# Dilated attention on one core: 64-row products and values' products as runs, PSUM banks shared otherwise

## The chip, the core and the metric

The kernel runs on one core of a Trainium2 chip. A core has a matrix engine (TensorE, PE here; its weight loads are shown apart as PEld), a vector engine (VectorE, DVE), a scalar engine (ScalarE, ACT), a general one (GpSimd, POOL) and one that issues transfers (SyncE, SP). Each takes its instructions in the order in which the program holds them and waits on semaphores. PE reads SBUF and writes PSUM, which has eight banks of 128 x 512 fp32. The metric is the device time of one execution in microseconds.

## The reference, cut to what matters

One decoder layer over 512 tokens of width 1024, in fp32: half a SwiGLU FFN, then three gated branches (an S5 state space model, causal dilated attention, cross attention into 256 memory tokens), an output projection, and a second half FFN. The change is in the dilated attention, and in the tags of the banks that the other two branches use.

```python
HEAD_DIM = 64
ATTN_PATTERNS = ((128, 1), (512, 4), (2048, 16))
HEADS_PER_PATTERN = 4

def dilated_mixture_attention(q, k, v, rel_table):
    ...
        logits = jnp.einsum('bqghd,bgqkhd->bghqk', qb, kb) * scale + bias[None, :, :, None, :]
        logits = jnp.where(valid[None, :, None], logits, -jnp.inf)
        lse = jax.nn.logsumexp(logits, axis=-1)
        probs = jnp.exp(logits - lse[..., None])
        out = jnp.einsum('bghqk,bgqkhd->bqghd', probs, vb)
        mix = jax.nn.softmax(lse, axis=1)
        return jnp.einsum('bghq,bqghd->bqhd', mix, out).astype(q.dtype)
```

The mixture over the three patterns, weighted by their softmax denominators, is one softmax over all keys of the three patterns together, and the kernel computes it so.

## The kernel before, in words

Tokens are held in residue order: token 4j + r stands at place j of block r, so a query tile is one of four blocks of 128 tokens (`r`), and the dilated patterns become dense products on blocks with a mask in the bias. Heads go in pairs (`hp`, two pairs): head 2hp lies on partitions 0 to 63, head 2hp + 1 on 64 to 127 of the transposed queries and keys. So there are eight tiles, `attn_tile(hp, r)`, of two heads each.

For one head of one tile, PE makes scores in two banks: `s0` (512 keys of the first pattern, by L856 over all 128 rows and L857 over the head's 64 rows, which adds the low part of the keys) and `s1` (128 keys of each of the other patterns, two products at L860 over 64 rows; an fp32 product shows as two passes in the profile). DVE adds the bias and takes the row maximum (L864, L866), L758 negates it, ACT takes the exponential with its sum (L762), DVE the reciprocal and the scaled row (L764, L765). PE transposes the row in six pieces of 128 (L873) into two banks, four pieces and two, and ACT copies them to `pt` (L874). When both heads have their `pt`, twelve products (L880), six key blocks times two heads, add up 64 columns each in `pacc`: one head's output on partitions 0 to 63, the other's on 64 to 127.

Between tiles, the program has the gated linear unit of the SSM branch and its gate (`up_block`, `gate_T`, with `mm_T`, L133 to L135): products of 128 rows by 512 columns, whose weights ACT and DVE split into high and low parts (L124, L125). After the eighth tile follow the gate of the attention branch and the product of its output `ath`/`atl` (`pacc`, split by L143 and L144) with `attn_w_up`.

PSUM, in this half of the kernel (`ps_open("ps_b", 2)`), has two banks each under the tags `mm`, `tr`, `sc` and `acc`. A tile under a tag waits until the one that held its bank before has been read.

The order of instructions on each engine is not that of the source. A scheduler takes, engine by engine, what it holds ready in a timeline of its own, with source order as priority; then the order is fixed, and an engine that meets a wait lets nothing by. `tc.issue_after(last)`, in the change, tells it to place an instruction behind another one.

Of the kernel before, what the change touches and what calls it, by code (L numbers as in the profile page):

```python
# [20 lines left out]
P = 128  # L21
T = 512
# [5 lines left out]
NEG = -1.0e30  # L28
# [56 lines left out]
def kernel(ctx, tc, x, mem, ffn1_norm, ffn1_w_in, ffn1_w_down, mix_norm, w_in, a_re, a_im, log_dt,  # L85
# [3 lines left out]
    V, S, G, TE = nc.vector, nc.scalar, nc.gpsimd, nc.tensor  # L89
# [570 lines left out]
    def ssm_units(pool, hd):  # L660

        MUL, ADD, SUB = ALU.mult, ALU.add, ALU.subtract
        for i in range(4):
# [16 lines left out]
            yield  # L680
            br = ps_tile("tr", 2)
            bi = ps_tile("tr", 2)
            for part, b in enumerate((br, bi)):
# [38 lines left out]
    def ssm_out(pool, i, stk, lt, ca, xr, xi):  # L722


        py = ps_tile("acc", 2)
        for q in range(4):
# [97 lines left out]
    def xattn_head(pool, hd, xq, mkT, mv):  # L824
        pts = [pool.tile([P, 2, T], F32R, name=f"xpt{z}", tag=f"xpt{z}", bufs=1) for z in "hl"]
        for r in range(4):
            s = ps_tile("sc", 2)
            tok = slice(r * P, (r + 1) * P)
            for i, (a, b) in enumerate(((0, 0), (0, 1), (1, 0))):
                TE.matmul(s[:, :256], xq[a][:, tok], mkT[hd][:, b], start=i == 0, stop=i == 2)  # L830
            mx = pool.tile([P, 1], F32, name="xmx", tag="xmx", bufs=2)
            V.tensor_reduce(mx, s[:, :256], axis=AX.X, op=ALU.max)
            pr = softmax_rows(s[:, :256], mx, pool, 128.0 ** -0.5, 256, "xa")
            pt = ps_tile("tr", 2)
            for kt in range(2):
                TE.transpose(pt[:, kt * P:(kt + 1) * P], pr[:, kt * P:(kt + 1) * P], ident)
            split_plain(pt[:, :256].rearrange("p (k q) -> p k q", k=2), pts[0][:, :, tok], pts[1][:, :, tok])
        po = ps_tile("tr", 2)
        cols = slice((hd % 2) * P, (hd % 2 + 1) * P)
# [8 lines left out]
    def attn_tile(pool, hp, r, qT, kT, v, bias, pacc):  # L848

        tok = slice(r * P, (r + 1) * P)  # L850
        pts = []
        for h in (2 * hp, 2 * hp + 1):
            rows = slice(64 * (h % 2), 64 * (h % 2) + 64)
            s0 = ps_tile("sc", 2)
            qs, (kh, kl) = qT[hp][h % 2], kT[hp]
            TE.matmul(s0, qs[:, tok], kh[h % 2], start=True, stop=False)  # L856
            TE.matmul(s0, qs[rows, tok], kl[rows, :], start=False, stop=True)  # L857
            s1 = ps_tile("sc", 2)
            for p in range(2):
                TE.matmul(s1[:, p * P:(p + 1) * P], qT[2 * p + 2 + hp][rows, tok], kT[2 * p + 2 + hp][rows, tok],  # L860
                          start=True, stop=True)
            sb = pool.tile([P, 6 * P], F32, name="sb", tag="sb", bufs=3)
            mx = pool.tile([P, 2], F32, name="amx", tag="amx", bufs=3)
            V.tensor_tensor_reduce(sb[:, :T], s0, bias[h][:, (3 - r) * P:(7 - r) * P], scale=1.0, scalar=NEG,  # L864
                                   op0=ALU.add, op1=ALU.max, accum_out=mx[:, 0:1])
            V.tensor_tensor_reduce(sb[:, T:], s1[:, :256], bias[h][:, 7 * P:9 * P], scale=1.0, scalar=mx[:, 0:1],  # L866
                                   op0=ALU.add, op1=ALU.max, accum_out=mx[:, 1:2])
            pr = softmax_rows(sb, mx[:, 1:2], pool, 1.0, 6 * P, "at", pr=sb)
            pt = pool.tile([P, 6, P], F32, name="pt", tag="pt", bufs=4)
            for b0, nb in ((0, 4), (4, 2)):  # L870
                ta = ps_tile("tr", 2)
                for b in range(nb):
                    TE.transpose(ta[:, b * P:(b + 1) * P], pr[:, (b0 + b) * P:(b0 + b + 1) * P], ident)  # L873
                S.activation(pt[:, b0:b0 + nb, :], ta[:, :nb * P].rearrange("p (k q) -> p k q", k=nb), AF.Copy)  # L874
            pts.append(pt)
        for b in range(6):
            for h in (2 * hp, 2 * hp + 1):
                rows = slice(64 * (h % 2), 64 * (h % 2) + 64)
                kt, c = (b, h * 64) if b < 4 else (r, (b - 3) * 256 + h * 64)
                TE.matmul(pacc[rows, tok], v[kt][:, c:c + 64], pts[h % 2][:, b, :], start=b == 0, stop=b == 5)  # L880

# [111 lines left out]
    with sb_pool("att") as ap:  # L993
# [8 lines left out]
        for hp in range(2):  # L1002
            pacc = ps_tile("acc", 2)
            for r in range(4):
# [304 lines left out]
```

## Time and profile before

| | |
|---|---|
| three runs | 1272.08 to 1273.12 us, median 1272.59 us |
| profiled execution | 1273.29 us, span 1271.5 us |
| PE busy | 1249.1 us, 98% of the span |
| DVE busy | 800.6 us, 63% |
| ACT busy | 474.9 us, 37% |
| chain that ended last | PE 92%, DVE 4%, DMA 2%, ACT 1% |
| attention stage | 654 to 804 us of the span |

Times in the profile are microseconds from the span's start. A row of a timeline has start, duration, engine, line, operation, output and inputs by the program's names, rows*columns of PE's array in use, shape and count; equal instructions that follow each other are one row. A row of a windows view has, for PE, PEld, DVE, ACT and POOL, busy time and count, then the clock granted to PE (1.00 is full), the share of time that the transfer engines were busy, and GB/s. A bracket at a row's end holds idle time ahead of it and what ended it.

### The profile page before, as it was taken

What the parts mean: (1) busy time and instruction counts of PE and PEld (TensorE: products, weight loads), DVE (VectorE), ACT (ScalarE), POOL (GpSimd) and SP (SyncE); (2) the same over time, 40 slices, a digit from 0 to 9 for tenths busy, and PEclk for the clock granted to TensorE, in tenths of its full rate; (3) what the DMA queues carried; (4) which work ended last, traced back from release to release, by engine and by line L of the source; (5) the groups of instructions that cost most, each with busy time, mean ns of one, the idle gap of its engine ahead of it and who ended that gap; (6) DMA issues with size and microseconds to landing.
All of it is one profiled execution on the core that took longest, in us unless ns stands there. A gap on an engine that the chain in (4) does not pass through costs nothing.

```text
span 1271.5 us, 17256 instructions
## 1 busy us (share of the span) xinstructions
PE 1249.1 (98%) x6764; PEld 1058.3 (83%) x6764; DVE 800.6 (63%) x1519; ACT 474.9 (37%) x744; POOL 104.8 (8%) x85
## 2 busy tenths in 40 slices
PE   8999999999999999999999999999998999999997
PEld 6788888788889788998877777888888899899896
DVE  7999456876547567745535455455588558558564
ACT  4322222233325333224423443334356335335343
POOL 3000000000012033420000000002200001001002
PEclk9999999999999999999999999999998999999999
DMA  6233333654227835652127221334645556556411
GB/s 198 86 114 117 132 106 103 174 162 148 94 88 247 262 117 171 176 169 81 53 70 152 67 67 42 100 108 142 185 105 130 144 152 163 141 149 168 132 66 67
DMA packets 167368, 163.60 MB, mean 129 GB/s; under 512 B 28244, under 2 KB 150676, under 8 KB 166996
## 3 DMA queue, kind: packets, MB, share of 16 engines
q1 hardware_dynamic: 134032, 138.20, 34.8%
q0 software_dynamic: 9632, 9.70, 5.2%
q10 hardware_dynamic: 23624, 14.61, 3.9%
q8 instruction: 53, 0.87, 0.3%
q14 instruction: 27, 0.22, 0.1%
HBM read 147.51 MB, written 16.16 MB: 129 GB/s over the span
## 4 chain that ended last, share of the span: by engine, by line
PE 92%; DVE 4%; DMA 2%; ACT 1%; issue 0%; SPq 0%; ACTq 0%
PE ps_mm L133 19%; PE ps_mm L135 19%; PE ps_mm L134 19%; PE ps_mm L1151 5%; PE ps_mm L1153 5%; PE ps_mm L1154 5%; PE ps_mm L1209 3%; PE ps_mm L1211 3%; PE ps_mm L1210 3%; DMA wraw<-in_xattn_w_kv_dram 1%; PE ps_acc L880 1%; DVE wl L125 1%; PE ps_mm L818 1%; PE ps_mm L817 1%; PE ps_mm L819 1%; PE ps_tr L873 1%
## 5 line engine op out<-in xcount | busy, mean ns | idle before, releaser
L124 ACT ACTIVATE wh<-wraw 128x1024 fp32r<-128x1024 f32 (+2 forms) x224 | 209.4, 937 | 482.3 <-PE ps_mm L134 347.2
L125 DVE TENSOR_TENSOR wl<-wraw,wh 128x1024 fp32r<-128x1024 f32 (+2 forms) x224 | 248.0, 1109 | 130.4 <-ACT wh L124 124.3
L133 PE MATMUL ps_mm<-uh,wh 128*128 128x512 f32 x736 | 289.9, 394 | 0.9 <-ACT uh L143 0.5
L134 PE MATMUL ps_mm<-ul,wh 128*128 128x512 f32 x736 | 288.2, 392 | 1.6 <-DVE ul L144 1.6
L135 PE MATMUL ps_mm<-uh,wl 128*128 128x512 f32 x736 | 288.5, 392 | 0.0
L133 PEld LDWEIGHTS ps_mm<-uh,wh 128*128 128x128 f32 x736 | 138.7, 188 | 30.7 <-issue 1.0
L134 PEld LDWEIGHTS ps_mm<-ul,wh 128*128 128x128 f32 x736 | 138.7, 188 | 30.6 <-DVE ul L144 1.9
L135 PEld LDWEIGHTS ps_mm<-uh,wl 128*128 128x128 f32 x736 | 138.5, 188 | 29.9 <-issue 0.7
L217 POOL TENSOR_TENSOR sqacc<-sqacc,sqk 128x512 f32<-128x512 f32 x12 | 20.1, 1678 | 694.5 <-ACT sqk L216 694.4
L125 DVE TENSOR_TENSOR wl<-s,wh 128x1024 fp32r<-128x1024 f32 x36 | 44.0, 1224 | 43.1 <-ACT wh L124 43.1
L134 PE MATMUL ps_mm<-gl,wh 128*128 128x512 f32 x176 | 70.0, 398 | 0.0
L133 PE MATMUL ps_mm<-gh,wh 128*128 128x512 f32 x176 | 69.9, 399 | 0.0
L135 PE MATMUL ps_mm<-gh,wl 128*128 128x512 f32 x176 | 69.8, 399 | 0.0
L1210 PE MATMUL ps_mm<-wl,gh 128*128 128x512 f32 x176 | 69.4, 394 | 0.0
L1211 PE MATMUL ps_mm<-wh,gl 128*128 128x512 f32 x176 | 69.1, 394 | 0.0
L1209 PE MATMUL ps_mm<-wh,gh 128*128 128x512 f32 x176 | 66.9, 395 | 0.0
L1151 PE MATMUL ps_mm<-uh,wh 128*128 128x256 f32 x216 | 61.1, 285 | 2.3 <-ACT uh L143 1.7
L124 ACT ACTIVATE wh<-s 128x1024 fp32r<-128x1024 f32 x36 | 38.2, 1061 | 64.3 <-PE ps_mm L1153 26.7
L1153 PE MATMUL ps_mm<-ul,wh 128*128 128x256 f32 x216 | 61.4, 285 | 0.7 <-DVE ul L144 0.7
L1154 PE MATMUL ps_mm<-uh,wl 128*128 128x256 f32 x216 | 61.0, 284 | 0.0
L143 ACT ACTIVATE gh<-ff_t 128x512 fp32r<-128x512 f32 x44 | 27.1, 626 | 56.7 <-DVE ff_t L312 33.4
L1151 PEld LDWEIGHTS ps_mm<-uh,wh 128*128 128x128 f32 x216 | 41.2, 191 | 2.9 <-ACT uh L143 2.1
(388 smaller groups left out, 2410.4 us busy)
## 6 DMA issues: line engine op xcount, KB each, us to landing
wraw<-in_ffn_w_in_dram SPq DMA_DIRECT2D x33, 1024.0 KB, 5.1
wraw<-in_w_in_dram SPq DMA_DIRECT2D x25, 1024.0 KB, 5.4
wraw<-in_ffn_w_down_dram SPq DMA_DIRECT2D x12, 768.0 KB, 4.3
s<-in_ffn_w_in_dram SPq DMA_DIRECT2D x18, 512.0 KB, 5.3
s<-in_ffn_w_in_dram POOLq DMA_DIRECT2D x18, 512.0 KB, 6.2
wraw<-in_ffn_w_down_dram SPq DMA_DIRECT2D x8, 1024.0 KB, 5.1
wraw<-in_ffn_w_down_dram SPq DMA_DIRECT2D x10, 512.0 KB, 3.5
q<-in_ffn_w_in_dram SPq DMA_DIRECT2D x9, 512.0 KB, 4.6
```

The lines of the kernel that those rows point to most:

```text
L124: S.activation(h, raw, AF.Copy)
L125: eng.tensor_tensor(l, raw, h.bitcast(F32), op=ALU.subtract)
L133: TE.matmul(ps, h[:, k, :], rhs[k][0], start=first and k == 0, stop=False)
L134: TE.matmul(ps, h[:, k, :], rhs[k][1], start=False, stop=False)
L135: TE.matmul(ps, l[:, k, :], rhs[k][0], start=False, stop=last and k == n - 1)
L143: S.activation(h, src, AF.Copy)
L1151: TE.matmul(o, h[:, k, cols], rhs[k][0], stop=False, **st)
L1153: TE.matmul(o, h[:, k, cols], rhs[k][1], stop=False, **st)
L1154: TE.matmul(o, l[:, k, cols], rhs[k][0], stop=k == 3, **st)
L1209: TE.matmul(pd[r], gh[:, tok], h, start=st, stop=False)
L1210: TE.matmul(pd[r], gh[:, tok], l, start=False, stop=False)
L1211: TE.matmul(pd[r], gl[:, tok], h, start=False, stop=en)
```

## The change

For a query tile, both heads' score banks are taken at once. PE makes the two full products, then the products over 64 rows in one sequence, chained with `issue_after`, with the heads in turn: the two 512-wide ones, then the two heads' first products for `s1`, then their second ones. The softmax of each head follows as before. The values' products begin with the last two key blocks, whose piece of `pt` is written last, and with the second head.

The banks are shared otherwise: `tr` is gone, `s1` is a tag of its own with two banks, `sc` has three (scores `s0`, transposed pieces, and outside the attention the SSM's output and the memory attention's scores and output), `acc` one (only `pacc`), `mm` two as before. Five lines are added ahead of L880, so later lines are five higher in the changed kernel: L857 makes the full products there, L865 all those over 64 rows, L878 transposes, L879 copies to `pt`, L885 multiplies the values.

```diff
--- before.py
+++ after.py
@@ -678,8 +678,8 @@
             for r in range(4):
                 nc.sync.dma_start(lt[0:32 * (r + 1), :, r, :], gd[32 * (3 - r):, 4 * i:4 * i + 4, :])
             yield
-            br = ps_tile("tr", 2)
-            bi = ps_tile("tr", 2)
+            br = ps_tile("s1", 2)
+            bi = ps_tile("s1", 2)
             for part, b in enumerate((br, bi)):
                 for q in range(4):
                     TE.matmul(b[:, q * P:(q + 1) * P], bl[:, part, q, :], stk[:, q, :], start=True, stop=True)
@@ -722,7 +722,7 @@
     def ssm_out(pool, i, stk, lt, ca, xr, xi):
 
 
-        py = ps_tile("acc", 2)
+        py = ps_tile("sc", 3)
         for q in range(4):
             for t, (lhsT, rhs) in enumerate(((lt[:, q], stk), (ca[:, 0, q], xr), (ca[:, 1, q], xi))):
                 TE.matmul(py[:, q * P:(q + 1) * P], lhsT.rearrange("p r c -> p (r c)"), rhs[:, q, :],
@@ -824,18 +824,18 @@
     def xattn_head(pool, hd, xq, mkT, mv):
         pts = [pool.tile([P, 2, T], F32R, name=f"xpt{z}", tag=f"xpt{z}", bufs=1) for z in "hl"]
         for r in range(4):
-            s = ps_tile("sc", 2)
+            s = ps_tile("sc", 3)
             tok = slice(r * P, (r + 1) * P)
             for i, (a, b) in enumerate(((0, 0), (0, 1), (1, 0))):
                 TE.matmul(s[:, :256], xq[a][:, tok], mkT[hd][:, b], start=i == 0, stop=i == 2)
             mx = pool.tile([P, 1], F32, name="xmx", tag="xmx", bufs=2)
             V.tensor_reduce(mx, s[:, :256], axis=AX.X, op=ALU.max)
             pr = softmax_rows(s[:, :256], mx, pool, 128.0 ** -0.5, 256, "xa")
-            pt = ps_tile("tr", 2)
+            pt = ps_tile("s1", 2)
             for kt in range(2):
                 TE.transpose(pt[:, kt * P:(kt + 1) * P], pr[:, kt * P:(kt + 1) * P], ident)
             split_plain(pt[:, :256].rearrange("p (k q) -> p k q", k=2), pts[0][:, :, tok], pts[1][:, :, tok])
-        po = ps_tile("tr", 2)
+        po = ps_tile("sc", 3)
         cols = slice((hd % 2) * P, (hd % 2 + 1) * P)
         for kt in range(2):
             for i, (a, b) in enumerate(((0, 0), (0, 1), (1, 0))):
@@ -849,35 +849,40 @@
 
         tok = slice(r * P, (r + 1) * P)
         pts = []
-        for h in (2 * hp, 2 * hp + 1):
-            rows = slice(64 * (h % 2), 64 * (h % 2) + 64)
-            s0 = ps_tile("sc", 2)
-            qs, (kh, kl) = qT[hp][h % 2], kT[hp]
-            TE.matmul(s0, qs[:, tok], kh[h % 2], start=True, stop=False)
-            TE.matmul(s0, qs[rows, tok], kl[rows, :], start=False, stop=True)
-            s1 = ps_tile("sc", 2)
-            for p in range(2):
-                TE.matmul(s1[:, p * P:(p + 1) * P], qT[2 * p + 2 + hp][rows, tok], kT[2 * p + 2 + hp][rows, tok],
-                          start=True, stop=True)
+        heads = (2 * hp, 2 * hp + 1)
+        s0 = [ps_tile("sc", 3) for _ in heads]
+        s1 = [ps_tile("s1", 2) for _ in heads]
+        kh, kl = kT[hp]
+        for e in range(2):
+            whole = TE.matmul(s0[e], qT[hp][e][:, tok], kh[e], start=True, stop=False)
+
+        last = whole.ins
+        rows = [(s0[e], qT[hp][e][halves[e], tok], kl[halves[e], :], False) for e in range(2)]
+        rows += [(s1[e][:, p * P:(p + 1) * P], qT[2 * p + 2 + hp][halves[e], tok], kT[2 * p + 2 + hp][halves[e], tok], True)
+                 for p in range(2) for e in range(2)]
+        for o, q, k, st in rows:
+            with tc.issue_after(last):
+                last = TE.matmul(o, q, k, start=st, stop=True).ins
+        for e, h in enumerate(heads):
             sb = pool.tile([P, 6 * P], F32, name="sb", tag="sb", bufs=3)
             mx = pool.tile([P, 2], F32, name="amx", tag="amx", bufs=3)
-            V.tensor_tensor_reduce(sb[:, :T], s0, bias[h][:, (3 - r) * P:(7 - r) * P], scale=1.0, scalar=NEG,
+            V.tensor_tensor_reduce(sb[:, :T], s0[e], bias[h][:, (3 - r) * P:(7 - r) * P], scale=1.0, scalar=NEG,
                                    op0=ALU.add, op1=ALU.max, accum_out=mx[:, 0:1])
-            V.tensor_tensor_reduce(sb[:, T:], s1[:, :256], bias[h][:, 7 * P:9 * P], scale=1.0, scalar=mx[:, 0:1],
+            V.tensor_tensor_reduce(sb[:, T:], s1[e][:, :256], bias[h][:, 7 * P:9 * P], scale=1.0, scalar=mx[:, 0:1],
                                    op0=ALU.add, op1=ALU.max, accum_out=mx[:, 1:2])
             pr = softmax_rows(sb, mx[:, 1:2], pool, 1.0, 6 * P, "at", pr=sb)
             pt = pool.tile([P, 6, P], F32, name="pt", tag="pt", bufs=4)
             for b0, nb in ((0, 4), (4, 2)):
-                ta = ps_tile("tr", 2)
+                ta = ps_tile("sc", 3)
                 for b in range(nb):
                     TE.transpose(ta[:, b * P:(b + 1) * P], pr[:, (b0 + b) * P:(b0 + b + 1) * P], ident)
                 S.activation(pt[:, b0:b0 + nb, :], ta[:, :nb * P].rearrange("p (k q) -> p k q", k=nb), AF.Copy)
             pts.append(pt)
-        for b in range(6):
-            for h in (2 * hp, 2 * hp + 1):
-                rows = slice(64 * (h % 2), 64 * (h % 2) + 64)
-                kt, c = (b, h * 64) if b < 4 else (r, (b - 3) * 256 + h * 64)
-                TE.matmul(pacc[rows, tok], v[kt][:, c:c + 64], pts[h % 2][:, b, :], start=b == 0, stop=b == 5)
+
+        for b in (4, 5, 0, 1, 2, 3):
+            for e in (1, 0):
+                kt, c = (b, heads[e] * 64) if b < 4 else (r, (b - 3) * 256 + heads[e] * 64)
+                TE.matmul(pacc[halves[e], tok], v[kt][:, c:c + 64], pts[e][:, b, :], start=b == 4, stop=b == 3)
 
     def up_block(raw, j, src):
         p = ps_tile("mm")
@@ -1000,7 +1005,7 @@
                 nc.sync.dma_start(bt[32 * g:32 * g + 32], src)
             bias.append(bt.rearrange("p s k -> p (s k)"))
         for hp in range(2):
-            pacc = ps_tile("acc", 2)
+            pacc = ps_tile("acc", 1)
             for r in range(4):
                 attn_tile(ap, hp, r, qT, kT, v, bias, pacc)
                 d = 4 * hp + r
```

The order that the scheduler makes of it, as read from the two programs. First PE, the scores of one tile (`kh`, `kl`, `qs`: high and low keys and queries; `kT`, `qT`: keys and queries of the other patterns), here one head of a tile of the second pair, before:

```order
L856 MATMUL ps_sc<-kh_4170,qs_4055 128x512
L857 MATMUL ps_sc<-kl_4172,qs_4055 128x512
L860 MATMUL ps_sc<-kT_4575,qT_4438 128x128
L860 MATMUL ps_sc<-kT_4912,qT_4836 128x128
L133 MATMUL ps_mm<-uh_97,wh 128x512
```

and after, both heads of such a tile:

```order
L878 MATMUL ps_sc<-ident,sb 128x128 x2
L857 MATMUL ps_sc<-kh_4170,qs_4055 128x512
L857 MATMUL ps_sc<-kh_4171,qs_4056 128x512
L865 MATMUL ps_sc<-kl_4172,qs_4055 128x512
L865 MATMUL ps_sc<-kl_4172,qs_4056 128x512
L865 MATMUL ps_s_6844<-kT_4575,qT_4438 128x128
L865 MATMUL ps_s_6845<-kT_4575,qT_4438 128x128
L865 MATMUL ps_s_6844<-kT_4912,qT_4836 128x128
L865 MATMUL ps_s_6845<-kT_4912,qT_4836 128x128
L133 MATMUL ps_mm<-uh_97,wh 128x512
```

The two heads' scores, which stood apart with ordinary products and another tile's work between, are one piece, and it follows the last transposes of the tile before. Of the 16 heads of before, 10 have their 64-row products in one piece as shown and 6 have L857 apart from L860; after, six of the eight tiles stand as shown, the first tile's 64-row products are in three pieces and the second's in two.

Second PE, the values' products of one tile (`v`: the values by block), before:

```order
L135 MATMUL ps_mm<-uh_104,wl 128x512
L880 MATMUL ps_acc<-pt,v_3968 64x128
L133 MATMUL ps_mm<-yh_3802,wh 128x512
```

```order
L135 MATMUL ps_mm<-yh_3808,wl 128x512
L880 MATMUL ps_acc<-pt,v_3968 64x128
L880 MATMUL ps_acc<-pt,v_3969 64x128 x2
L880 MATMUL ps_acc<-pt,v_3970 64x128 x2
L880 MATMUL ps_acc<-pt,v_3971 64x128 x6
L133 MATMUL ps_mm<-uh_97,wh 128x512
```

and after:

```order
L133 MATMUL ps_mm<-uh_101,wh 128x512
L885 MATMUL ps_acc<-pt,v_3969 64x128 x4
L885 MATMUL ps_acc<-pt,v_3968 64x128 x2
L885 MATMUL ps_acc<-pt,v_3969 64x128 x2
L885 MATMUL ps_acc<-pt,v_3970 64x128 x2
L885 MATMUL ps_acc<-pt,v_3971 64x128 x2
L134 MATMUL ps_mm<-ul_109,wh 128x512
```

In all eight tiles one product stood alone, ahead of a run of eleven; now there are twelve in one run.

Third, the end of the stage, with the seventh and the eighth tile. On PE after, from the eighth tile's last score product on:

```order
L865 MATMUL ps_s_6988<-kT_4912,qT_4836 128x128
L885 MATMUL ps_acc<-pt,v_3970 64x128 x4
L885 MATMUL ps_acc<-pt,v_3968 64x128 x2
L885 MATMUL ps_acc<-pt,v_3969 64x128 x2
L885 MATMUL ps_acc<-pt,v_3970 64x128 x2
L885 MATMUL ps_acc<-pt,v_3971 64x128 x2
L878 MATMUL ps_sc<-ident,sb 128x128 x12
L885 MATMUL ps_acc<-pt,v_3971 64x128 x4
L885 MATMUL ps_acc<-pt,v_3968 64x128 x2
L885 MATMUL ps_acc<-pt,v_3969 64x128 x2
L885 MATMUL ps_acc<-pt,v_3970 64x128 x2
L885 MATMUL ps_acc<-pt,v_3971 64x128 x2
```

Ahead of these rows stand the seventh tile's twelve transposes and, directly behind them, the eighth tile's eight score products, of which the last is the first row here; behind them stands one product of `ath` (L133 ath_7123), and then the next gate's block. Before, 13 ordinary products stood between the last transposes and the last values, and 24 behind those. On ACT, after, the same stretch (L879 copies to `pt`, L762 exponentials, L143 copies `pacc` to `ath`, L747 is a gate's tanh, which frees the bank that the next gate's block takes):

```order
L124 ACTIVATE wh<-wraw 128x256
L879 ACTIVATE pt<-ps_sc 128x512
L879 ACTIVATE pt<-ps_sc 128x256
L879 ACTIVATE pt<-ps_sc 128x512
L879 ACTIVATE pt<-ps_sc 128x256
L762 ACTIVATE sb,atsm<-sb,atnm 128x768 x2
L879 ACTIVATE pt<-ps_sc 128x512
L879 ACTIVATE pt<-ps_sc 128x256
L879 ACTIVATE pt<-ps_sc 128x512
L879 ACTIVATE pt<-ps_sc 128x256
L143 ACTIVATE ath_7123<-ps_acc 128x512
L747 ACTIVATE gate<-ps_mm 128x512
```

The first attention gate's block stands ahead of all these rows on PE now, and its tanh directly behind `ath` on ACT; before, that block stood behind the last values. On DVE the two heads' biased maxima (L869, L871 after) stand together, then the two negations, then each head's reciprocal and scaled row.

## The prediction

> **What bounds the kernel now.** I read the page's busy shares and chain first, then the stage that the change touches, by windows and as a timeline of TensorE (PE).
>
> ```profile
> PE 1249.1 (98%) x6764; PEld 1058.3 (83%) x6764; DVE 800.6 (63%) x1519; ACT 474.9 (37%) x744; POOL 104.8 (8%) x85
> PE 92%; DVE 4%; DMA 2%; ACT 1%; issue 0%; SPq 0%; ACTq 0%
> 700.00:750.00 50.00, 50.00 (x303) 37.87 (x303) 25.50 (x69) 22.82 (x45) 0.00 (x0) 1.00 0.20 64
> PE ps_mm L133 <- DVE mg L990: 0.3, 1, 0.3
> ```
>
> PE is the chain, and in the middle of the attention stage it is busy for all 50 us while DVE and ACT work half of it. The last row is the only wait that the profile gives PE between 654 and 804 us. So PE's time there is the kernel's time, and what the change saves on PE comes off the end, as long as it makes no new waits. But "busy" hides something; the timeline shows it (start, duration, line, rows*columns of the array in use, count):
>
> ```profile
> 684.95 0.39 PE L135 MATMUL ps_mm<-yh,wl 128*128 128x512 f32 x1
> 685.18 0.39 PE L856 MATMUL ps_sc<-kh,qs 128*128 128x512 f32 x1
> 685.50 0.50 PE L857 MATMUL ps_sc<-kl,qs 64*128 64x512 f32 x1
> 685.84 0.60 PE L860 MATMUL ps_sc<-kT,qT 64*128 64x128 f32 x4
> 686.37 0.50 PE L133 MATMUL ps_mm<-yh,wh 128*128 128x512 f32 x1
> 686.70 0.39 PE L134 MATMUL ps_mm<-yl,wh 128*128 128x512 f32 x1
> ...
> 697.68 0.40 PE L856 MATMUL ps_sc<-kh,qs 128*128 128x512 f32 x1
> 698.01 0.50 PE L857 MATMUL ps_sc<-kl,qs 64*128 64x512 f32 x1
> 698.44 0.50 PE L135 MATMUL ps_mm<-uh,wl 128*128 128x512 f32 x1
> 698.77 0.40 PE L133 MATMUL ps_mm<-yh,wh 128*128 128x512 f32 x1
> ...
> 704.16 0.40 PE L134 MATMUL ps_mm<-yl,wh 128*128 128x512 f32 x1
> 704.48 0.71 PE L860 MATMUL ps_sc<-kT,qT 64*128 64x128 f32 x4
> 705.12 0.51 PE L135 MATMUL ps_mm<-yh,wl 128*128 128x512 f32 x1
> 705.46 0.39 PE L133 MATMUL ps_mm<-yh,wh 128*128 128x512 f32 x1
> ```
>
> A 512-wide product over 128 rows starts 0.23 us after the one before (684.95 to 685.18). Where PE goes from 128 rows to 64, or back, the next starts are late: 0.32 into the run, 0.34 after its first product, then 0.33 after the first product back on 128 rows. A visit to the 64-row shape therefore costs some 0.4 us beside its products.
>
> **The change, part by part, in PE time.**
>
> *Products over 64 rows.* One head's run, from L856 (685.18) to L134 (686.70), is 1.52 us; less two ordinary starts (L856 itself and L133) it is 1.05. Split in two by the order, it is 697.68 to 698.77 (1.09 less 0.47, so 0.62) for L857, and 704.16 to 705.46 (1.30 less 0.47, so 0.83) for the L860 pair: 1.45. In the program of before 10 of the 16 heads stand whole and 6 split: 10 x 1.05 + 6 x 1.45 = 19.2 us.
>
> In the changed order six tiles have one run each: L857's form for both heads, then four L860 products, heads in turn. Heads use rows 0 to 63 and 64 to 127. No row of this trace has two row halves in turn, so the price is bounded by the nearest rows: in L860 x4 with one half a pass starts each (0.60 - 0.27)/3 = 0.11 us, and L880 with two column halves in turn (below) starts one each 0.06, two at a time. If row halves go like column halves, the run for two heads takes no longer than one head's: 1.05. If they don't, the second L857 adds 0.23 and four more passes 0.44: 1.72. I take 1.05, since L880 is the same array cut the other way, and each head here writes a bank of its own. The first tile is split in three (two L857 0.62, three products 0.83, one 0.62: 2.1) and the second in two (0.62 + 0.83, less 0.15 for a switch that it shares with the values: 1.3). Sum after 6 x 1.05 + 3.4 = 9.7, gain 9.5 us; without overlap it is 14.9, gain 4.3.
>
> [...]
>
> *The values' products.* Before, the scheduler always put one of the twelve alone and eleven in a run:
>
> ```profile
> 794.95 0.39 PE L135 MATMUL ps_mm<-uh,wl 128*128 128x512 f32 x1
> 795.27 0.43 PE L880 MATMUL ps_acc<-pt,v 128*64 128x128 f32 x2
> 795.63 0.50 PE L133 MATMUL ps_mm<-yh,wh 128*128 128x512 f32 x1
> 795.97 0.39 PE L134 MATMUL ps_mm<-yl,wh 128*128 128x512 f32 x1
> ...
> 714.26 1.52 PE L880 MATMUL ps_acc<-pt,v 128*64 128x128 f32 x22
> ```
>
> The single one costs 794.95 to 795.97, 1.02 less 0.47, so 0.55 us. The run of eleven is 22 passes in 1.52 us, (1.52 - 0.27)/21 = 0.06 a pass; they run in pairs, so a twelfth product fits beside the eleventh for nothing. Eight tiles: 8 x 0.55 = 4.4 us gained. Saved on PE: 9.5 + 4.4 = 13.9 us.
>
> *The new waits.* From the third tile on, 27 to 33 ordinary products and the values of the tile before lie between a tile's scores and its transposes: 27 x 0.23 + 1.6 = 7.8 us at least, 9.2 mostly. The softmax of two heads has these rows (DVE, then ACT):
>
> ```profile
> 787.93 0.69 DVE L864 CUSTOM_DVE_ANT_0 sb<-ps_sc,bias 128x512 f32<-128x512 f32 x1
> 788.55 0.08 DVE L864 DVE_READ_ACCUMULATOR2_ANT amx<- 128x1 f32 x1
> 790.83 0.48 DVE L866 CUSTOM_DVE_ANT_0 sb<-ps_sc,bias,amx 128x256 f32<-128x256 f32 x1 [1.60 <-PE ps_sc L860]
> 791.24 0.08 DVE L866 DVE_READ_ACCUMULATOR2_ANT amx<- 128x1 f32 x1
> 791.36 0.15 DVE L758 TENSOR_SCALAR atnm<-amx 128x1 f32<-128x1 f32 x1
> 792.67 0.16 DVE L764 RECIPROCAL atri<-atsm 128x1 f32<-128x1 f32 x1 [1.16 <-ACT sb L762]
> 792.87 0.62 DVE L765 TENSOR_SCALAR sb<-sb,atri 128x768 f32<-128x768 f32 x1
> 791.61 0.94 ACT L762 ACTIVATE sb<-sb,atnm 128x768 f32<-128x768 f32 x1 [0.76 <-DVE atnm L758]
> 789.97 0.87 ACT L874 ACTIVATE pt<-ps_tr 128x512 f32<-128x512 f32 x2 [3.40 <-PE ps_tr L873]
> 789.28 0.87 PE L873 MATMUL ps_tr<-ident,sb 128*128 128x128 f32 x6
> 803.64 0.60 ACT L143 ACTIVATE ath<-ps_acc 128x512 fp32r<-128x512 f32 x1 [0.57 <-PE ps_acc L880]
> ```
>
> From a score's start: 0.5 to the end of the product, 2 x 0.62 and 2 x 0.41 for the biased maxima, 0.1 and 0.25 to the exponential, 1.06 to the reciprocal, 0.2 and 0.62 to the scaled row: 4.8 us for the first head, 5.9 for the second, and one or two gate products or weight splits stand between on DVE. Counted from the run's start, 0.9 us earlier than its end, there are 2.8 us and more to spare, so in these tiles PE does not wait. The fourth transposing bank waits for the first copy, but stands 15 products later, 3.5 us, against 0.69 + 0.6.
>
> At the end of the stage this cover is gone. There the transposes of the seventh tile, the scores of the eighth, the values of the seventh, the transposes of the eighth, its values and the product of the new `ath` stand on PE one behind the other, where before 13 products (3.0 us) stood between the last transposes and values, and 24 behind. Clock from the first of these transposes:
> - three banks serve four transposed pieces and two scores. Copies begin at 0.69, a pair takes 0.87, so the scores' banks are free at 1.56 and 2.1 where PE would want them at 1.3 and 1.5: 0.5 us waited.
> - the small products start at 2.4, the run ends and the values of the seventh tile go from 3.3 to 4.7. The scaled row of the eighth tile comes at 2.4 + 4.8 = 7.2: 2.5 waited. The second head's at 8.3, PE free at 7.9: 0.4 waited.
> - its last pair of copies goes from 8.3 + 0.69 to 9.85; the values could have started at 9.1: 0.75 waited.
> - the values' last pass starts at 11.1, the copy to `ath` ends 0.3 + 0.6 later, 12.0, wanted at 11.3: 0.7. The next product needs the bank that L747's tanh frees, which stands behind this copy on ACT: 0.15 more.
>
> Sum 5.0 us of waiting, in under 11 us. This moves PE's granted clock, by these windows (columns as above, the clock next to last but two):
>
> ```profile
> 418.70:422.10 3.40, 1.70 (x6) 1.21 (x7) 3.40 (x7) 1.32 (x4) 0.00 (x0) 1.00 1.02 320
> 422.10:425.50 3.40, 3.40 (x9) 2.67 (x9) 2.39 (x4) 1.04 (x2) 0.14 (x2) 0.50 0.97 331
> 466.50:469.90 3.40, 2.14 (x15) 1.67 (x15) 1.89 (x3) 3.28 (x5) 3.40 (x4) 1.00 0.83 259
> 954.60:958.00 3.40, 1.50 (x8) 1.09 (x8) 3.37 (x9) 3.15 (x9) 0.00 (x0) 1.00 0.59 228
> 958.00:961.40 3.40, 2.96 (x13) 2.66 (x13) 3.40 (x12) 2.89 (x7) 0.00 (x0) 0.50 0.00 0
> 961.40:964.80 3.40, 3.40 (x16) 3.11 (x16) 3.40 (x9) 1.36 (x5) 0.00 (x0) 0.50 0.23 71
> ```
>
> Where PE worked 1.70 or 1.50 of 3.4 us, the next 3.4 or 6.8 us ran at half the clock; after 2.14 they did not. The wait from 4.7 to 7.2 leaves less than 1 of 3.4. Half clock for 3.4 to 6.8 us costs at most 1.7 to 3.4 us, and nothing while PE waits for others anyway; between 0 and 3.4 I take 2.0.
>
> *PSUM banks elsewhere.* The SSM and the memory attention get other tags with as many or more buffers; their PE order is the same but for a few places inside the memory attention, where 24 to 28 ordinary products still stand between a score and its transposes. I cost them at nothing; the cover is those products, 5.6 us.
>
> Sum: 13.9 - 5.0 - 2.0 = 6.9 us. The profiled execution took 1273.29 us (span 1271.5), so 1266.4; the median of the three runs is 0.7 lower, which gives **1265.7 us**.
>
> **Rivals.**
> - *No half clock.* The saving stays at 13.9 - 5.0 = 8.9: 1263.7. It needs the waits to straddle two windows with 2 us of work in each. Against it: the rows at 418.7 and 954.6, both with shorter waits than 2.5. [...]
> - *The two row halves do not overlap* (the change merges runs but doesn't do what "in turn" is for). The gain is 4.3 + 4.4 = 8.7; the end of the stage waits 0.2 longer: 8.7 - 5.2 - 2.0 = 1.5, so 1271.1, no measurable change; with no half clock 1269.1. For it: no row here shows two row halves at once. Against it: column halves do overlap.
> - *Slower: the transposes wait in every tile.* The scores of two heads now enter DVE's queue together, with weight splits and gate products between them, and PE stands behind the second head's scaled row. If the 5.9 us grew until PE waited 2 us in each tile, the seven tiles ahead of the last would lose 14 us: 1265.7 + 14 = 1279.7. It decides from (6.9 + 2.5)/7 = 1.3 us of wait a tile on. For it: DVE and ACT serve one queue each in order, and wait for each other. Against it: DVE is busy for 25.5 of 50 us, and the 2.8 us to spare.
>
> **How the numbers follow.** The forecast has 0.53, with its own range 1263 to 1269; no half clock 0.16; no overlap 0.18; slower 0.13. About 0.2% (2.5 us) is what can be told from no change. Faster by that: 0.53 + 0.16 + 0.03 of the third, 0.72. Same: 0.15. Slower: 0.13. The range goes from 1261.5 (no half clock and 2 us less of waiting) to 1272.0, past the third case, and leaves the last one out.
>
> **What would show it.** In the profile after: a run of both heads' small products as one group, with about as long from first to last start as one head's had (0.34 + 0.53 us); if it is 0.67 longer, they don't overlap. The values x24 in 1.52 us. PE waits at the end of the stage, near 790 us: on the row scaling (L765) 2.5 us, on the copies (L879) about 1.2, on `ath` 0.7, and a window of 3.4 to 6.8 us at clock 0.50 behind. No PE waits on L765 in earlier tiles. It would be wrong if those waits are missing, if PE waits in the memory attention, or if the single run costs more than 1.05 us.

## The result, and the profile after

The changed kernel takes 1265.33 us (median of four runs, 1264.72 to 1267.81) against 1272.41 us for the kernel before beside it: a ratio of 0.9948, 95% interval 0.9936 to 0.9961. It is faster by 7.1 us; 1265.7 was predicted. The profiled execution is the one of 1264.72 us. First the busy times and the chain on its page:

```profile
PE 1236.0 (98%) x6764; PEld 1052.0 (83%) x6764; DVE 798.7 (63%) x1519; ACT 474.5 (38%) x744; POOL 104.8 (8%) x85
PE 91%; DVE 5%; DMA 3%; ACT 1%; issue 1%; SPq 0%; ACTq 0%; DVEq 0%
```

PE works 13.1 us less for the same 6764 products, and is still the chain. Yet the span fell by only 8.6 us. The timeline of PE, around the sixth tile's run and the values behind it, shows what was saved:

```profile
778.46 0.71 PE L857 MATMUL ps_sc<-kh,qs 128*128 128x512 f32 x2
779.10 0.50 PE L865 MATMUL ps_sc<-kl,qs 64*128 64x512 f32 x2
779.44 0.60 PE L865 MATMUL ps_s<-kT,qT 64*128 64x128 f32 x8
779.98 0.51 PE L133 MATMUL ps_mm<-uh,wh 128*128 128x512 f32 x1
780.32 0.40 PE L134 MATMUL ps_mm<-ul,wh 128*128 128x512 f32 x1
...
783.19 1.53 PE L885 MATMUL ps_acc<-pt,v 128*64 128x128 f32 x24
```

Two heads' products over 64 rows go from 779.10 to 779.98, 0.34 + 0.54 us: as long as one head's before. Eight passes take the 0.60 us of four. All twelve products of the values stand in one run of 1.53 us.

The waits of PE in the attention stage and behind it (in total, times, longest), then its timeline at the end of the stage:

```profile
PE ps_sc L878 <- DVE sb L765: 2.4, 1, 2.4
PE ps_mm L133 <- ACT ath L143: 0.7, 1, 0.7
PE ps_acc L885 <- ACT pt L879: 0.5, 1, 0.5
PE ps_mm L133 <- DVE mg L995: 0.3, 1, 0.3
```

```profile
788.02 1.72 PE L878 MATMUL ps_sc<-ident,sb 128*128 128x128 f32 x12
789.58 0.98 PE L857 MATMUL ps_sc<-kh,qs 128*128 128x512 f32 x2
790.49 0.51 PE L865 MATMUL ps_sc<-kl,qs 64*128 64x512 f32 x2
790.84 0.61 PE L865 MATMUL ps_s<-kT,qT 64*128 64x128 f32 x8
791.37 1.53 PE L885 MATMUL ps_acc<-pt,v 128*64 128x128 f32 x24
795.34 2.73 PE L878 MATMUL ps_sc<-ident,sb 128*128 128x128 f32 x12 [2.44 <-DVE sb L765]
798.61 1.62 PE L885 MATMUL ps_acc<-pt,v 128*64 128x128 f32 x24 [0.53 <-ACT pt L879]
800.93 0.50 PE L133 MATMUL ps_mm<-ath,wh 128*128 128x512 f32 x1 [0.70 <-ACT ath L143]
```

Only the last row of the waits was there before. The other three are new, all between 792 and 801 us, where the last tile ends: nothing stands any more between the seventh tile's values and the eighth's transposes. The twelve transposes at 795.34 take 2.73 us, those at 788.02 took 1.72. The windows view (granted clock last but two) says why:

```profile
792.02:795.43 3.41, 0.97 (x19) 0.76 (x14) 2.24 (x11) 1.95 (x4) 0.00 (x0) 1.00 0.33 123
795.43:798.84 3.41, 2.88 (x14) 2.48 (x16) 0.65 (x2) 1.74 (x4) 0.00 (x0) 0.50 0.08 31
```

**Where the 8.6 us come from.** For lengths, take as the stage the time from the first L830 product of the memory attention to the last product that reads `ath`: 571.90 to 858.36 before, 570.93 to 849.84 after. It became 7.55 us shorter. Another 0.97 us lies ahead of it, and behind it nothing changed. What lies ahead took 569.35 to 571.90 us in the ten executions profiled here, whatever the kernel: PE's clock becomes full between 11.0 and 14.3 us (before, 512-wide products start 0.43 us apart from 10.12 to 11.83 and 0.22 apart from 12.61 on), and in five of the ten a stretch of 3.41 us at half clock stands near 420 us (before, 422.13 to 425.54). So the length of the stage is given below beside the medians; half a microsecond shows in it that the medians can't tell. It comes from one execution of each kernel, so a stretch at half clock in it is that execution's. "The end of the stage" stays the end of the attention tiles, from some 788 to 804 us.

### The profile page after: what moved, and what is told of

It reads as the page before. It is cut to its first block, busy times and chain, and to the rows that moved or that the text cites. A ratio compares the mean times of both kernels' runs of the same rounds, so it can differ in the third digit from the quotient of the medians.

```text
span 1262.9 us, 17246 instructions
## 1 busy us (share of the span) xinstructions
PE 1236.0 (98%) x6764; PEld 1052.0 (83%) x6764; DVE 798.7 (63%) x1519; ACT 474.5 (38%) x744; POOL 104.8 (8%) x85
## 4 chain that ended last, share of the span: by engine, by line
PE 91%; DVE 5%; DMA 3%; ACT 1%; issue 1%; SPq 0%; ACTq 0%; DVEq 0%
PE ps_mm L133 19%; PE ps_mm L134 19%; PE ps_mm L135 19%; PE ps_mm L1158 5%; PE ps_mm L1159 5%; PE ps_mm L1156 5%; PE ps_mm L1214 3%; PE ps_mm L1215 3%; PE ps_mm L1216 3%; DVE wl L125 1%; PE ps_mm L817 1%; PE ps_sc L878 1%; PE ps_mm L819 1%; PE ps_mm L818 1%; PE ps_sc L728 1%; DMA wraw<-in_ffn_w_in_dram 1%
## 5 line engine op out<-in xcount | busy, mean ns | idle before, releaser
L133 PE MATMUL ps_mm<-uh,wh 128*128 128x512 f32 x736 | 289.6, 394 | 0.9 <-ACT uh L143 0.6
L133 PEld LDWEIGHTS ps_mm<-uh,wh 128*128 128x128 f32 x736 | 138.3, 188 | 30.6 <-ACT uh L143 1.0
L133 PE MATMUL ps_mm<-gh,wh 128*128 128x512 f32 x176 | 70.0, 399 | 0.0
L143 ACT ACTIVATE gh<-ff_t 128x512 fp32r<-128x512 f32 x44 | 27.1, 627 | 55.4 <-DVE ff_t L312 31.9
```

Source lines behind the costliest of these rows:

```text
L133: TE.matmul(ps, h[:, k, :], rhs[k][0], start=first and k == 0, stop=False)
L143: S.activation(h, src, AF.Copy)
```

## The experiments

Ratios are to the kernel before, run beside each group on the same chip (1271.95 us for the first four, 1271.56 us for the last four). "Stage" is the stage of the profiled execution: 286.46 us before, 278.91 after.

| kernel | median us | ratio, 95% | stage us |
|---|---|---|---|
| the change, heads one after the other | 1266.46 | 0.9956 (0.9943 to 0.9969) | 280.32 |
| the change, values in the old order | 1268.34 | 0.9970 (0.9959 to 0.9980) | 283.93 |
| before, banks alone | 1281.20 | 1.0070 (1.0059 to 1.0082) | 297.17 |
| before, values' order alone | 1266.12 | 0.9952 (0.9940 to 0.9964) | 281.70 |
| the change, a gate in the long wait | 1261.48 | 0.9918 (0.9902 to 0.9934) | 275.87 |
| the same, its tanh early | 1260.55 | 0.9908 (0.9891 to 0.9925) | 275.21 |
| the change, spare products in the wait | 1262.94 | 0.9937 (0.9914 to 0.9960) | 278.01 |
| the change, a gate in three waits | 1259.11 | 0.9898 (0.9882 to 0.9914) | 274.06 |

### Do the two row halves work at once?

The edit (two lines shortened by "..."):

```diff
-        rows = [(s0[e], qT[hp][e][halves[e], tok], kl[halves[e], :], False) for e in range(2)]
-        rows += [(s1[e][:, p * P:(p + 1) * P], ..., True) for p in range(2) for e in range(2)]
+        rows = []
+        for e in range(2):
+            rows += [(s0[e], qT[hp][e][halves[e], tok], kl[halves[e], :], False)]
+            rows += [(s1[e][:, p * P:(p + 1) * P], ..., True) for p in range(2)]
```

> The changed kernel, with one thing taken back: inside the run of 64-row products the first head's three stand ahead of the second head's three, where the change has the two heads in turn. The order of everything else on PE is that of the changed kernel, so the runs are as few and stand in the same places. Theory (the two row halves of the array work at the same time): each of the six whole runs grows by 0.67 us, less one pass of 0.11 us where the second head's first product meets the first head's last, 0.56, so 3.4 us; the two split tiles add up to 0.4 each. The time goes from 1265.3 to about 1269 (1268.5 to 1270), and the timeline shows 0.5 to 0.67 us more between the first product of a run and the first product behind it. Rival (the gain is only that there are fewer visits to the 64-row shape): runs as long as in the changed kernel and 1265.3, within 0.5.

Measured: 1266.46 us, below the range expected; 1.1 us slower than the change by the medians, which their spread can't tell from none; the stage 1.41 us longer. The timeline of the sixth tile's run:

```profile
781.29 0.50 PE L867 MATMUL ps_sc<-kl,qs 64*128 64x512 f32 x1
781.63 0.27 PE L867 MATMUL ps_s<-kT,qT 64*128 64x128 f32 x1
781.64 0.50 PE L867 MATMUL ps_sc<-kl,qs 64*128 64x512 f32 x1
781.74 0.84 PE L867 MATMUL ps_s<-kT,qT 64*128 64x128 f32 x7
782.51 0.50 PE L133 MATMUL ps_mm<-uh,wh 128*128 128x512 f32 x1
```

The run is 1.22 us, 781.29 to 782.51, against 0.88 in turn: 0.34 longer in each of the six whole runs, not 0.56. So the halves do work at once, and the rival (runs as long) falls, but the theory mis-sized it. The second head's wide product is the fourth in the program, with three passes of the first head still ahead of it, and yet it starts 0.01 us after the first head's first narrow pass. PE, as recorded, lets one half run ahead of the other by itself, and the order in turn only gets the last third of a microsecond. So with products on different row halves the recorded starts are not in the order in which the program holds the products. Two halves in turn take 0.88 us where one head's took 0.87, so twice the work in the same time.

The runs alone would make the stage longer by 2.1 us, and with the two split tiles the times from the start of each 64-row product to the next start add up to 10.5 us against 7.8. The stage is only 1.41 longer because of its end. There this kernel waits 2.1 us for the row scaling, but its clock stays full:

```profile
793.17:796.59 3.42, 2.59 (x34) 2.17 (x34) 2.31 (x10) 0.76 (x1) 0.00 (x0) 1.00 0.02 5
796.59:800.00 3.41, 1.76 (x12) 1.26 (x12) 1.57 (x4) 2.66 (x8) 0.00 (x0) 1.00 0.45 154
```

The boundary at 796.59 cuts the wait (795.8 to 797.85) in two. PE is busy for 2.59 us of the one window and 1.76 us of the other, and the clock is 1.00 in both and in the window behind them (800.00 to 803.41).

### The values' order, taken back and alone

Taken back in the change (here and in the next edit the product's start and stop flags move with the order; that line isn't shown):

```diff
-        for b in (4, 5, 0, 1, 2, 3):
-            for e in (1, 0):
+        for b in range(6):
+            for e in (0, 1):
```

> The changed kernel with the values' twelve products in the order of the kernel before (blocks 0 to 5, first head first). Their order lets one of them start before the rest has its operands, so in seven of eight tiles they stand in two or three pieces again: four tiles as one product, 15 to 33 others, eleven; the others with the pieces next to 64-row products or transposes. Theory (a visit by values alone costs 0.55 us, as the prediction has it, and a piece that stands beside another change of shape costs less): 4 to 5 lone pieces at 0.55 are 2.2 to 2.8 us, the pieces beside others 0 to 1, so 1267.5 to 1269. At the end of the stage one lone product and a split run stand between the last transposes, which shortens nothing there. Rival (the values' order is worth nothing, the run of 64-row products is the whole gain): 1265.3 within 0.7.

Alone, on the kernel before:

```diff
-        for b in range(6):
-            for h in (2 * hp, 2 * hp + 1):
+        for b in (4, 5, 0, 1, 2, 3):
+            for h in (2 * hp + 1, 2 * hp):
```

> The kernel before with nothing changed but the order of the values' products (blocks 4, 5, 0 to 3, second head first). All eight tiles then have their twelve in one run, 20 to 28 ordinary products still stand ahead of the last transposes and values at the end of the stage, and the heads' 64-row products stay apart. Theory (a lone product costs 0.55 us, a twelfth beside the eleventh nothing): 8 x 0.55 = 4.4 us less, 1268.0 (1267.5 to 1269), with PE's busy time 4 us lower and no wait on the row scaling. If that is so, then the rest of the change is worth 9.5 - 7 = 2.7 us net. Rival (the lone product costs nothing because the next one was ready to go anyway): 1272.4 within 0.7.

Both times came out as the theory has it. Taken back, 3.0 us of median are lost and 5.0 us of stage: 3.1 ahead of the eighth tile's first score product, and 1.9 behind it, where this execution had two windows at half clock, one more than the change. The order isn't the expected one, though. Only one tile has one product, others and eleven; in four tiles the values stand as nine products and three, on both sides of a run of 64-row products:

```profile
766.40 1.31 PE L885 MATMUL ps_acc<-pt,v 128*64 128x128 f32 x18
767.64 0.73 PE L857 MATMUL ps_sc<-kh,qs 128*128 128x512 f32 x2
768.30 0.51 PE L865 MATMUL ps_sc<-kl,qs 64*128 64x512 f32 x2
768.65 0.61 PE L865 MATMUL ps_s<-kT,qT 64*128 64x128 f32 x8
769.18 0.65 PE L885 MATMUL ps_acc<-pt,v 128*64 128x128 f32 x6
```

Alone, the stage is 4.76 us shorter, where 4.4 was expected. The median fell by 5.8; 2.55 us of what the profiled execution gained lie ahead of the stage, where it had no stretch at half clock. All eight tiles have one run (the last one's row is below), and PE's only wait in the stage is the one that was there before:

```profile
797.24 1.53 PE L880 MATMUL ps_acc<-pt,v 128*64 128x128 f32 x24
```

```profile
PE ps_mm L133 <- DVE mg L990: 0.3, 1, 0.3
```

So the order of the values, without any of the rest, gives by the medians within the error the time of the whole change (1266.12 against 1265.33 us). The stage tells them apart: 281.70 against 278.91 us, so the rest of the change is worth 2.8 us net (the expectation's 9.5 - 7 is 2.5). In the profiled executions 1.6 us of it are hidden by what lies ahead of the stage (569.35 against 570.93 us). Most of what the rest saves on PE it loses again at the stage's end.

### The banks alone

The edit is the tags of the diff (`sc` 3, `s1` 2, `acc` 1, no `tr`) on the kernel before, and no other line.

> The kernel before with nothing changed but which work shares which PSUM banks (three for scores and transposed pieces, two for the small scores, one for the values' sums, none of their own for transposes). The scores of a head then wait for other banks, and nearly every head's 64-row products come apart into two or three visits. Theory (a visit to another shape costs 0.4 us whatever the reason): some ten heads more stand split, 10 x 0.4 = 4 us, and at the end of the stage the products that stood between the transposes and the values are gone, as in the changed kernel, 4 to 6 us of waiting and half clock; so 1278 to 1284, slower than before. Rival (the banks by themselves are free, as the prediction has them, or bring part of the gain): 1272.4 or less.

9.3 us slower, as expected, but not by the parts expected. The heads' products stand in three pieces a tile, of which one joins two heads, and the values in two: 40 visits in all against 36 before. Those that hold no wait cost only some 0.7 us more than before, by their starts, where 4 us were expected. The stage is 10.7 us longer, so nearly all of it is lost at the end, which has two long waits and four windows at half clock (the waits, then the window ahead of those four and the first of them):

```profile
PE ps_sc L873 <- DVE sb L765: 5.1, 2, 3.0
```

```profile
804.45:807.86 3.41, 1.30 (x8) 0.98 (x8) 0.79 (x2) 1.66 (x4) 0.00 (x0) 1.00 0.43 154
807.86:811.27 3.41, 0.88 (x3) 0.29 (x2) 1.85 (x7) 1.26 (x3) 0.00 (x0) 0.50 0.00 0
```

Sharing the banks by itself is a cost, not a gain: it takes away the cover at the end of the stage. In these runs it pays only together with the merged runs that it makes room for; merged runs with the banks as before were not run.

### Is the end of the stage time given back?

Four kernels fill the waits of the change. The first computes the first two gates behind the attention ahead of their use, the second one's 24 products behind the seventh tile's values (of this edit and the next three, the main lines):

```diff
...
+                if (hp, r) == (1, 2):
+                    seventh = values
...
-        g = op.tile([P, T], F32, name="gate", tag="gate", bufs=2)
-        gate_T(d, 1, g)
+        if d == 0:
+            early = [gate_T(0, 1, op.tile([P, T], F32, name="gate", tag="gate", bufs=2))]
+            with tc.issue_after(seventh):
+                early.append(gate_T(1, 1, op.tile([P, T], F32, name="gate", tag="gate", bufs=2)))
+        g = early[d] if d < 2 else gate_T(d, 1, ...)
```

> The changed kernel, with other work put into its long wait at the end of the stage: the first two gates of the projection behind the attention are computed ahead of their use, and the second one's 24 products (24 x 0.23 = 5.6 us) stand on PE behind the seventh tile's values, where PE waited 2.4 us for the row scaling and then worked 3.4 us at half clock. Nothing is left out. Theory (those waits are time that the change gave back): the 2.4 us and the net 0.8 us of half clock go, the clock stays at 1.00 there, but the gates' tanh stands on ACT behind the copy to ath and holds a bank, so the first product of ath waits 1.3 instead of 0.7 us: 1265.3 - 3.2 + 0.6 = 1262.7 (1262 to 1264). Rival (the wait moves: the transposes wait for the row scaling all the same, or the two gates computed early hold up something else): 1265.3 within 0.7.

The second puts the tanh of these two gates ahead of the copy to `ath` on ACT:

```diff
...
-        S.activation(g, p, AF.Tanh, scale=0.5)
+        with tc.high_priority(1500 if b == 1 and d < 2 else 0):
+            S.activation(g, p, AF.Tanh, scale=0.5)
```

> As the kernel with the gate in the wait, and the tanh of the two gates stands on ACT ahead of the copy to ath. Theory: the first product of ath waits 0.7 to 0.9 us as in the changed kernel; the 2.4 us, the half clock (0.8) and the 0.15 behind the tanh are gone, the second head's transposes now wait some 0.4 as they run at full clock: 1265.3 - 3.0 = 1262.3 (1261.5 to 1263.3), below the kernel with the late tanh by 0.4. Rival (the time behind the wait doesn't count): 1265.3 within 0.7.

The third has eight products into a free bank in place of the gate:

```diff
...
+        if behind is not None:
+            spare = ps_tile("s1", 2)
+            for _ in range(8):
+                with tc.issue_after(behind):
+                    behind = TE.matmul(spare, qT[hp][0][:, tok], kh[0], start=True, stop=True).ins
```

> The changed kernel with eight spare 512-wide products behind the seventh tile's values, whose result nothing reads: 8 x 0.23 = 1.9 us of work within the 2.4 us that PE waits. Nothing is left out. It tells what the half clock costs by itself. Theory (PE's granted clock halves behind a window in which it was busy for less than about 1.7 of 3.4 us): with the spare products the window is busy for about 2.8, the clock stays at 1.00, the twelve transposes start every 0.11 us again instead of every 0.21, which is 1.2 us, of which 0.4 comes back as a wait of the second head's: 0.8 us earlier, 1264.5 (1264.0 to 1265.3), although PE does more. Rival (the clock halves whatever PE does in that wait): transposes every 0.21 us and 1265.3 or more.

The fourth splits the gate's products:

```diff
...
+            for k in range(KD):
+                with tc.issue_after(behind[0][1] if k < 4 else behind[1][0] if k < 5 else behind[1][1]):
+                    for i, (a, b) in enumerate(((h, 0), (h, 1), (l, 0))):
+                        TE.matmul(p, a[:, k, :], U[k][b], start=k == 0 and i == 0, stop=k == KD - 1 and i == 2)
```

> As the kernel with the gate in the wait and its tanh early, but the gate's 24 products in three parts, one for each wait at the end of the stage: 12 (2.8 us) behind the seventh tile's values, 3 (0.7 us) behind the eighth's transposes, 9 (2.1 us) behind the eighth's values. Nothing is left out. Theory (each of these waits is on the path, and any product that is ready fills it): 2.4 for the row scaling, 0.8 of half clock, 0.5 for the copies and 0.7 + 0.15 for ath go, 0.4 may remain for the second head: 1265.3 - 4.3 = 1261.0 (1260.3 to 1262), faster than the changed kernel and than each of the other two fillings. Rival (only the long wait counts, the shorter ones come back elsewhere): as the one with the early tanh, 1262.3.

The stages are 3.04, 3.70, 0.90 and 4.85 us shorter than the change's, where 2.6, 3.0, 0.8 and 4.3 were expected: the sums hold, and the rivals fall. The medians are 3.9, 4.8, 2.4 and 6.2 us lower than the change's, and stand 0.5 to 1.2 us below the ranges expected. The kernel before, too, took 0.85 us less beside these four than beside the change, which would make most of this; the rest isn't placed.

With the gate in it, the long wait is gone. With the late tanh the row behind the values reads:

```profile
803.27 0.50 PE L133 MATMUL ps_mm<-ath,wh 128*128 128x512 f32 x1 [1.18 <-ACT gate L747]
```

With the early tanh this row has no such wait, and the stage is 0.66 us shorter again. The 0.7 us that were expected there for `ath` didn't come either: six products of the first pair's `ath` and `atl` stand behind the values, from 801.13 to 802.63, and the copy to the second pair's `ath` ends at 801.85. With the spare products PE does 1.85 us more, and is done 0.90 us earlier (its timeline, then windows):

```profile
791.85 2.12 PE L870 MATMUL ps_s<-kh,qs 128*128 128x512 f32 x8
794.27 1.80 PE L883 MATMUL ps_sc<-ident,sb 128*128 128x128 f32 x12 [0.30 <-DVE sb L765]
796.81 1.53 PE L890 MATMUL ps_acc<-pt,v 128*64 128x128 f32 x24 [0.74 <-ACT pt L884]
```

```profile
791.40:794.80 3.40, 3.10 (x23) 2.23 (x20) 2.19 (x10) 1.95 (x4) 0.00 (x0) 1.00 0.44 154
794.80:798.20 3.40, 2.61 (x34) 2.03 (x31) 0.34 (x1) 1.74 (x4) 0.00 (x0) 1.00 0.00 0
```

The transposes take 1.80 us where the change's took 2.73, and the clock is full: 0.90 us, from these two executions, is the net price of the half clock in the change. With the gate in three parts no wait is left at the end of the stage, as its timeline and its waits have it:

```profile
794.65 1.73 PE L879 MATMUL ps_sc<-ident,sb 128*128 128x128 f32 x12
796.13 0.47 PE L1054 MATMUL ps_mm<-uh,wh 128*128 128x512 f32 x1
...
797.00 1.53 PE L886 MATMUL ps_acc<-pt,v 128*64 128x128 f32 x24
798.46 0.50 PE L1054 MATMUL ps_mm<-uh,wh 128*128 128x512 f32 x1
...
800.63 0.40 PE L133 MATMUL ps_mm<-ath,wh 128*128 128x512 f32 x1
```

```profile
PE ps_mm L133 <- DVE mg L997: 0.3, 1, 0.3
```

This kernel beats both: 1259.11 us (1258.58 to 1259.56), 1.0% under the kernel before, its interval below that of the change.

## Why the prediction was right, step by step

- **What bounds it.** Right. PE remained the chain, and its starts make up the stage.
- **Saved on PE, 13.9 us.** Right. Price each visit to a shape of half the array as from the last start ahead to the second start behind, less two ordinary starts (0.23 us for a 512-wide product, 0.11 for a transpose), and sum over the stage: 36 visits with 36.6 us before, 16 with 22.9 us in the kernel with a gate in three waits, which has the change's runs and no waits. That is 13.7 us. For the 64-row products it is 9.8 (9.5 predicted): six whole runs at 1.07 to 1.16 us and the split tiles. For the values it is 3.9 (4.4 predicted). The twelfth product was free, as predicted: between ordinary products the run of 22 before (801.75 to 803.87) and that of 24 after (782.87 to 784.99) both take 2.12 us from start to start, a price of 1.65. The half microsecond lies in what stands beside the runs: where a transpose followed, as in seven tiles before, the run of 22 cost 1.60. The eight lone products had cost 4.4.
- **Row halves overlap.** Right, and 779.10 to 779.98 is the row that was asked for. The rival's 1.72 us is the price without any overlap, which no run shows: even with the heads apart a run cost 1.42, because the halves overlapped by themselves (781.63 and 781.64 there). So the order in turn, which that rival calls the means to the overlap, is worth 2.1 us here and not the 4 that its price gives for six runs. The prediction also went by each head's bank of its own; no run varied that.
- **Waits at the end of the stage, 5.0 us.** Right place, right order. Row scaling 2.44 (2.5), copies 0.53 (0.75), `ath` 0.70 (0.7), each by its row above; the banks for the scores 0.6 (0.5): 788.02 to 790.49 is 2.47 us, where eleven transposes of 0.11 and the 0.64 of 778.46 to 779.10 make 1.85; the bank behind the tanh 0.26 (0.15), 800.93 to 801.42 less an ordinary start. The second head's wait (0.4) didn't come, because at half clock the first head's transposes took longer; with the spare products, at full clock, the second head's transposes do start some 0.2 us late. Sum 4.5.
- **Half clock, 2.0 us.** Mis-sized. It came where it was placed, for one window, and cost 0.90 net. Full, it would be 1.1 us for twelve transposes (eleven starts at 0.21 in place of 0.11 us), and 0.1 of the values (1.62 against 1.53); part of that covered the second head's wait. The first rival's condition, waits that straddle two windows, is real: it is what the run with the heads apart shows (2.09 us of waiting cut at 796.59, clock 1.00 behind).
- **Given back in all, 7.0 us.** 13.7 - 7.55 = 6.15 by the stage. The rows above explain 5.4 of it; 0.7 isn't placed.
- **PSUM banks elsewhere, nothing.** Right for the memory attention: PE has no new wait there. But the sharing is by no means free in the attention itself: alone it costs 9.3 us. The prediction counted that cost, as the waits and the half clock at the end.
- **Slower rival (transposes wait in every tile).** It fell: PE waits for the scaled row once.
- **What hid in the sum.** That the median, 1265.33, is within 0.4 us of the forecast is in part luck. The stage gained 7.55 us where 6.9 were forecast: the half clock was 1.1 and the waits 0.5 too dear, against 0.2 too much saved and the 0.7 that isn't placed. Another 0.97 us of the profiled execution lies ahead of the stage, where the change has no part in it, so that execution (1264.72) is 1.7 us below the 1266.4 that the sum gives for it. The median doesn't show this because the profiled execution of before was 0.7 us above its median, and that of the change was the fastest of its four, 0.6 us below.

## What to carry to other kernels

Price every change of the array's shape as a visit (0.55 us for a lone product here), and count the visits in the order that the scheduler makes: an accumulation order that lets the whole run become ready at once removes visits for nothing (eight here, 4.8 us of the stage). When runs are merged, look at the last iteration, where there is no work of the next one to hide the latency; ready work put there gave 4.9 us of the stage more, where the whole change had given 7.6. Where PE has to wait, work without use can still be cheaper than the clock that it loses: 1.85 us of it made the stage 0.90 us shorter here.

## What the runs showed of the hardware

- The clock granted to PE changes at boundaries 3.41 us apart in these traces (792.02, 795.43 and 798.84 are some of this kernel's). In the executions of before and after, from 15 to 1250 us, each window on this grid in which PE was busy for less than 1.75 us was followed by half clock: 0.97 and 1.21 (from 792.02 and 945.61) here, 1.73 and 1.49 before (1.70 and 1.50 in the prediction's windows). So were 1.29 (values in the old order) and 1.30 (banks alone). That 1.75 is no sharp bound. 1.76 (heads apart), 1.80 (the change, from 416.56) and 2.15 (the change, from 464.34) weren't followed by it; but 1.85 (spare products), 1.90 (values in the old order) and 2.33 (banks alone), all near 945 to 968 us, were; and 1.55 at the very end of the run with the spare products wasn't. So the busy share of a window doesn't by itself tell what follows; what else counts wasn't settled. The first of these exceptions, as windows:

```profile
944.55:947.96 3.41, 1.85 (x10) 1.43 (x10) 3.38 (x10) 3.00 (x9) 0.00 (x0) 1.00 0.45 175
947.96:951.38 3.42, 2.98 (x13) 2.53 (x12) 3.42 (x11) 3.07 (x8) 0.00 (x0) 0.50 0.00 0
```

- A wait of 2.44 us within one window (the change) cost a window at half clock, one of 2.09 us cut by a boundary (heads apart) cost none. How many windows follow (one, two, or four in the kernel with the banks alone) wasn't settled. PE didn't have to be idle for a whole window: 1.73 us of work in 3.41 were followed by half clock (before, from 418.72).
- Transposes too run at half pace under it: twelve in 2.73 us, so a start every 0.21 us, against ten in 1.25 us, a start every 0.11, at 773.74 in the change.
- The two row halves of the array each take their own products, start 3 to 8 ns apart in turn (L865 in the change), and one half can run ahead of the other's place in the program (as recorded: 781.64 against 781.74 to 781.96 for the other half's next three passes, with the heads apart).
